# Attention sums and outputs stored from SyncE's queue, and two portions of a unit put inside the attention's first and third quarter

## The chip, the cores and the metric

The kernel runs on 1 core of one Trainium2 chip. The metric is the device time of the program in microseconds (us). The kernel before takes 651.97 us, the median of 3 runs (651.77 to 652.3).

## What is computed

One layer of a hybrid block over 1024 latent tokens and 256 context tokens of width 1024. Cut to what matters:

```python
h  = rmsnorm(x, norm_g) * (1 + scale) + shift          # scale, shift, gate = silu(c) @ w_ada + b_ada
hc = rmsnorm(ctx, norm_g) * (1 + scale_c) + shift_c
q, k, v, za, u, bg, cg, zc = split(h @ w_in)           # eight groups of 512 columns
kc, vc = split(hc @ w_in[:, 512:1536])
# 8 heads of 64: q, k normalised; 8x16 clamped window with a bias table, rotary on latent scores,
# all 256 context keys in the same softmax
attn = neighbourhood_attention(q, k, v, kc, vc, rpb) * silu(za)
conv = bg * conv3(cg * u) * silu(zc)
x_new = x + gate * (concat([attn, conv]) @ w_out)
```

Everything is float32. A product is made of three matmuls (high by high, high by low, low by high), for which each operand is split into a rounded high part and the rest.

## The kernel before, in words

**Stages.** The program first makes the modulated rows `h` (held on the chip as pairs of high and low, tiles `h`), then projects q, k and v in 32 tiles of 128 tokens (`proj_tile`, tile `pacc`) and spills them to DRAM. The attention follows, and then the output projection (`pout`, lines 74 to 76 by way of `out_mm`). The other columns of the input projection (`za`, and `u`, `cg`, `zc`, `bg` of the convolution) are not a stage of their own. They are 16 units of 128 columns, which fill TensorE in and around the attention.

**A unit** (`unit`, lines 338 to 363) is a product of 128 columns with all 1024 tokens: two halves of 512 tokens, each a PSUM bank `pu` (tag U, two banks) that eight steps of k accumulate. Two steps of k, six matmuls of 128x512, are one *portion*; a unit has eight. `next(fill)` issues one portion and stops ahead of the next. With its first portion a unit loads the weights of the next one (`unit_load`, two tiles `uraw` of 256 KB, SyncE's queue), and with its fourth and sixth it queues their splits into `uh` (on ScalarE) and `ul` (on VectorE). The end of a unit queues what is done with its result: for the four `za` units and the `zc` units a SiLU (`silus`, tile `zs`), for the others products of the convolution on VectorE.

**The attention** (lines 1267 to 1295) is a software pipeline of 36 calls of `quarter(n)`, n from 0 to 35. A head has four quarters. In quarter n TensorE makes the scores of quarter n (`pss` against latent keys, `pc` against context keys), the maxima of quarter n-2 are turned and spread (two transposes of `mx` into `pmx`, a VectorE maximum `rm`, two transposes that spread `rm`, a ScalarE copy `mg`), the exponentials of quarter n-2 are taken (`phc`, `phl` and their rests `plc`, `pll`), and the products with v of quarter n-3 are made (`po`). `e = n - 2` and `o = n - 3` are the two older quarters, and `live` says whether such a quarter exists. So quarters 0 and 1 have no maxima to turn, and quarters 0 to 2 have no products with v.

Portions lie between these: one after the exponentials are issued, and `TICKS[n] - 1` more at the end of the quarter, 3 a quarter in most. Ahead of the attention 8 portions have been issued; what is left after quarter 35 is issued in one row (line 1289), ahead of the output projection.

**The order on each engine.** Within the attention the program order of TensorE, ScalarE, VectorE and GpSimd is kept (`strict`, class `ordered`); DMA issues of ScalarE are free of that chain, and SyncE's queue is not in the list, so a scheduler orders its DMAs. [...]

**The stores.** When the last product with v of a bank of 512 queries is issued, `finish` (lines 1019 to 1024) copies the bank `po` (64 rows of outputs and one row of sums) into `ob`, of which there is one buffer, and stores the sums to `rs_d` (2 KB) and the outputs to `o_d` (128 KB). There are 16 such pairs of stores, in quarters 5, 7, 9 and so on. Both are issued from ScalarE. The sums of a pair of heads come back on SyncE's queue (`gated`, line 1250) to be inverted, and the last pair's on GpSimd's queue (`recip`, line 501).

## Time and profile before

| | |
|---|---|
| time, median of 3 runs | 651.97 us |
| the profiled execution: its own time, and the span of its trace | 651.68 us, 649.9 us |
| TensorE busy | 629.0 us, 97% of the span |
| VectorE, ScalarE, GpSimd busy | 431.9, 322.6, 129.4 us |
| moved by DMA | 125.46 MB, mean 193 GB/s |
| the attention in the span | about 279 to 543 us; the output projection starts at 558.22 us |

Times in the trace count from the start of the span. PE is TensorE, PEld its weight loads, DVE VectorE, ACT ScalarE, POOL GpSimd; SPq and ACTq are the queues on which SyncE and ScalarE issue DMAs. A row of a timeline has start, duration, engine, line, operation, output<-input, shape and count, and in brackets how long the engine sat idle before it and what ended that. Busy matmuls are counted to their modelled ends, so that a short wait can lie under the tail of the matmul ahead of it.

### The profile page before, as it was taken

The numbers are of one execution on the slowest core, as the hardware profiler recorded it, in microseconds if no ns is written. First come the engines' busy times: TensorE is split into PE (matmuls) and PEld (weight loads), VectorE is DVE, ScalarE is ACT, GpSimd is POOL, SyncE is SP. The second block draws the span as 40 slices with busy tenths as digits, with TensorE's granted clock in tenths as the row PEclk, the third lists the DMA queues.
The fourth block names the chain that finished last, engine by engine and source line by source line (L and its number), as shares of the span: only waits on it lengthen the run. The fifth ranks groups of instructions, "written<-read, shape, count | busy, mean of one in ns | idle before, by whom it ended". The sixth has DMA issues, their size and how long they took to land.

```text
span 649.9 us, 10273 instructions
## 1 busy us (share of the span) xinstructions
PE 629.0 (97%) x3469; PEld 539.2 (83%) x3469; DVE 431.9 (66%) x814; ACT 322.6 (50%) x693; POOL 129.4 (20%) x137
## 2 busy tenths in 40 slices
PE   5799999999999999999999999999999999999997
PEld 1467799899899999977877888888888888888885
DVE  1557774966684856457786889988998864575111
ACT  3466653442553635428677558565685645352000
POOL 1203203312222132101121111111211111004321
PEclk9799999999999999999999999999999999999999
DMA  8854637686686898789939576886782223966521
GB/s 321 314 179 166 168 105 243 202 263 196 196 278 177 251 262 254 187 228 218 241 103 238 145 179 191 211 213 153 207 190 75 74 75 118 324 222 222 178 102 50
DMA packets 118864, 125.46 MB, mean 193 GB/s; under 512 B 32817, under 2 KB 89353, under 8 KB 117532
## 3 DMA queue, kind: packets, MB, share of 16 engines
q1 hardware_dynamic: 112348, 113.23, 60.9%
q10 hardware_dynamic: 6208, 11.05, 5.3%
q0 software_dynamic: 256, 0.54, 0.3%
q8 instruction: 27, 0.44, 0.3%
q14 instruction: 25, 0.20, 0.1%
HBM read 88.01 MB, written 38.53 MB: 195 GB/s over the span
## 4 chain that ended last, share of the span: by engine, by line
PE 72%; DMA 7%; DVE 7%; ACT 5%; SPq 4%; issue 2%; POOL 1%; ACTq 0%; DVEq 0%; POOLq 0%
PE pu L55 22%; PE pacc L55 17%; PE po L55 5%; PE pout L74 4%; PE pout L75 4%; PE pout L76 4%; SPq L55 3%; PE tr L55 3%; PE cacc L55 3%; PE pss L55 2%; PE pmx L55 2%; DMA v<-v_d 2%; DMA k_s<-k_d 2%; PE pc L55 2%; DVE mx L55 2%
## 5 line engine op out<-in xcount | busy, mean ns | idle before, releaser
L55 PE MATMUL pu<-h,uh 128*128 128x512 f32 x544 | 169.0, 392 | 0.0
L55 PE MATMUL pacc<-wh,h 128*128 128x384 f32 x512 | 135.1, 338 | 0.0
L55 PEld LDWEIGHTS pu<-h,uh 128*128 128x128 f32 x544 | 98.2, 188 | 17.0
L55 PE MATMUL pu<-h,ul 128*128 128x512 f32 x272 | 106.3, 391 | 0.0
L55 PEld LDWEIGHTS pacc<-wh,h 128*128 128x128 f32 x512 | 92.9, 188 | 0.1
L55 POOL TENSOR_TENSOR plc<-sc,phc 128x512 fp32r<-128x512 f32 x32 | 42.5, 1328 | 221.9 <-ACT sc L55 113.2
L55 PE MATMUL pacc<-wl,h 128*128 128x384 f32 x256 | 85.6, 335 | 0.0
L55 POOL TENSOR_TENSOR ss<-ss,few 128x4 f32<-128x4 f32 (+1 forms) x40 | 42.0, 1051 | 126.9 <-DVE ss L55 126.5
L55 PEld LDWEIGHTS pu<-h,ul 128*128 128x128 f32 x272 | 51.1, 188 | 11.2
L55 DVE TENSOR_TENSOR mx<-mx,sb 128x384 f32<-128x384 f32 (+1 forms) x64 | 55.1, 869 | 2.0
L75 PE MATMUL pout<-wol,yh 128*128 128x512 f32 x128 | 49.8, 389 | 0.0
L76 PE MATMUL pout<-woh,yl 128*128 128x512 f32 x128 | 49.6, 389 | 0.0
L74 PE MATMUL pout<-woh,yh 128*128 128x512 f32 x128 | 48.3, 389 | 0.0
L55 PEld LDWEIGHTS pacc<-wl,h 128*128 128x128 f32 x256 | 48.1, 188 | 0.1
L55 DVE TENSOR_REDUCE ss<-sq 128x4 f32<-128x260 f32 (+1 forms) x40 | 15.7, 393 | 46.0 <-ACT sq L55 45.0
L55 ACT COPY mg<-pmx 128x256 f32<-128x256 f32 x32 | 12.0, 374 | 57.8 <-PE pmx L55 47.2
L55 ACT ACTIVATE sq<-pacc 128x256 f32<-128x256 f32 x32 | 12.3, 386 | 53.1 <-PE pacc L55 52.3
L1355 DVE TENSOR_TENSOR ot<-pout,gate 128x512 f32<-128x512 f32 x16 | 10.8, 688 | 40.2 <-PE pout L76 37.7
L55 DVE TENSOR_TENSOR pll<-sb,phl 128x768 fp32r<-128x768 f32 (+2 forms) x33 | 29.3, 889 | 7.9 <-ACT sb L55 7.9
L1356 POOL TENSOR_TENSOR ot<-ot,xr 128x512 f32<-128x512 f32 x15 | 19.6, 1315 | 68.6 <-DVE ot L1355 67.6
L55 DVE TENSOR_TENSOR sc<-sc,mg 128x512 f32<-128x512 f32 x32 | 21.8, 683 | 17.1 <-ACT mg L55 17.1
L55 ACT ACTIVATE qn<-pacc,ss 128x64 f32<-128x64 f32 x128 | 30.1, 330 | 6.0 <-POOL ss L55 3.2
(146 smaller groups left out, 1276.0 us busy)
## 6 DMA issues: line engine op xcount, KB each, us to landing
uraw<-in_w_in SPq DMA_DIRECT2D x34, 256.0 KB
q_d<-qs SPq DMA_DIRECT2D x64, 128.0 KB
k_s<-k_d SPq DMA_DIRECT2D x16, 512.0 KB
q_s<-q_d SPq DMA_DIRECT2D x32, 256.0 KB
wr<-in_w_in SPq DMA_DIRECT2D x40, 192.0 KB
slab<-in_w_ada SPq DMA_DIRECT2D x6, 1024.0 KB
t_d<-btw SPq DMA_DIRECT2D x8, 576.0 KB
bt<-t_d SPq DMA_DIRECT2D x8, 576.0 KB
```

Of the source, the lines that this page charges most:

```text
L55: i = emit(*a, **kw)
L74: i = pe.matmul(ps, ah, bh, start=first, stop=False)
L75: pe.matmul(ps, ah, bl, start=False, stop=False)
L76: pe.matmul(ps, al, bh, start=False, stop=last)
L1355: dve.tensor_tensor(ot, ps, gate[:, cols], ALU.mult)
L1356: (dve if (nh, t) == (1, NB - 1) else pool).tensor_tensor(ot, ot, xr, ALU.add)
```

## The change

The two stores of `finish` are issued by SyncE in place of ScalarE. In quarter 2 (the only one that turns maxima and has no product with v yet) a portion stands between the transposes of `mx` and those of `rm`. In quarter 0 a portion stands between the latent scores and the context scores. `TICKS` stays, so all later portions stand two places earlier, and two fewer are left after quarter 35.

```diff
@@ finish
             act.copy(ob[0:HD + 1], self.po[bank][0:HD + 1])
-            act.dma_start(rs_d[self.p][self.s, bank:bank + 1], ob[64:65])
-            act.dma_start(o_d[self.p][64 * self.s:64 * self.s + 64, bank * 512:(bank + 1) * 512], ob[0:64])
+            sp.dma_start(rs_d[self.p][self.s, bank:bank + 1], ob[64:65])
+            sp.dma_start(o_d[self.p][64 * self.s:64 * self.s + 64, bank * 512:(bank + 1) * 512], ob[0:64])
@@ quarter
         if gating and next(gating[0], "end"):
             gating.clear()
         if live(e):
+            if not live(o):
+                next(fill)
             for i in range(2):
                 pe.transpose(pm[:, 256 + i * P:256 + (i + 1) * P], rm[:, i:i + 1].broadcast_to([P, P]), ident)
             act.copy(mg[:, g * 256:(g + 1) * 256], pm[:, 256:512])
         now = pair_of(n)
         for i, hd_, j in now:
             hd_.scores(j, sbank[:, i])
+        if n == 0:
+            next(fill)
         if live(n):
             heads[n // 4].ctx_scores(n % 4)
```

## The prediction

> **What bounds the kernel now.** I read the page first: busy shares and the granted clock.

> ```profile
> span 649.9 us, 10273 instructions
> PE 629.0 (97%) x3469; PEld 539.2 (83%) x3469; DVE 431.9 (66%) x814; ACT 322.6 (50%) x693; POOL 129.4 (20%) x137
> ...
> PE   5799999999999999999999999999999999999997
> ...
> PEclk9799999999999999999999999999999999999999
> ```

> TensorE is busy for 97% of the span at full granted clock, and the few slices that are not full lie at the two ends. So the kernel is bound by TensorE's instruction stream, and a change can gain only where TensorE stands idle, or by taking matmuls away. This change takes none away. The next view is the windows, cut at the stages.

> ```profile
> 277.00:293.00 16.00, 14.43 (x77) 12.15 (x76) 8.43 (x17) 4.60 (x9) 0.00 (x0) 1.00 0.91 230
> 293.00:365.00 72.00, 69.03 (x389) 56.54 (x388) 56.59 (x86) 52.65 (x84) 13.53 (x12) 1.00 0.79 192
> 365.00:541.00 176.00, 175.72 (x1012) 149.54 (x1011) 153.98 (x236) 108.74 (x180) 29.17 (x26) 1.00 0.61 156
> 541.00:600.00 59.00, 59.00 (x264) 48.86 (x263) 33.15 (x51) 22.70 (x37) 10.46 (x12) 1.00 0.69 229
> ```

> The second number is the length, the third TensorE's busy time. Its idle time is 1.57 us in the attention's first three quarters, 2.97 us in the next 72 us, 0.28 us in the remaining 176 us, and nothing at the start of the output projection. The whole attention holds 4.82 us to be won. The third view, the timeline, says what the idle time waits for.

> ```profile
> 279.26 0.48 PE L55 MATMUL pss<-q_s,k_s 128*128 128x256 f32 x2
> 280.80 0.74 PE L55 MATMUL pc<-q_s,kc_s 128*128 128x256 f32 x4 [1.05 <-DVE qs L55]
> ...
> 289.40 0.38 PE L55 MATMUL pmx<-ci,mx 128*128 128x128 f32 x2
> 290.29 0.43 PE L55 MATMUL pmx<-ci,rm 128*128 128x128 f32 x2 [0.52 <-DVE rm L55]
> ```

> These two waits are the 1.57 us of the first window. In quarter 0 the context scores wait for VectorE to finish with the banks they need. In quarter 2 the spreading transposes wait for the maximum of the transposes just made. They are exactly where the change puts its portions.

> **The portions.** The chain of waits shows what a portion costs, in the row that is left at the end:

> ```profile
> 543.41 14.97 PE pu L55 x66
> ```

> That is eleven portions of six matmuls, 14.97 / 11 = 1.36 us each. In quarter 0 the two `pss` matmuls, half as wide as a portion's, take 1.36 / 6 = 0.23 us together (an estimate). A portion from 279.49 ends at 280.85, and `pc` starts 0.05 us later than before, so 1.31 of 1.36 us is hidden. In quarter 2 between 0.52 us (the idle time shown) and 0.89 us (all the way from 289.40 to 290.29) is hidden; I take 0.66, since the transposes' own issue lies in the 0.89. As `TICKS` stays, two portions fewer follow quarter 35, where TensorE has no idle time and each costs its full 1.36 us. So the two together win 1.31 + 0.66 = **1.97 us**. The idle rows give 1.05 + 0.52 = 1.57 us, less, because they begin only at the modelled tail of the matmul ahead.

> The moved portions need their operands earlier:

> ```profile
> 275.06 0.65 ACT L55 ACTIVATE zs<-pu 128x512 f32<-128x512 f32 x1
> 276.58 1.29 DVE L55 TENSOR_TENSOR ul<-uraw,uh 128x512 fp32r<-128x512 f32 x2
> 278.89 0.60 ACT L55 ACTIVATE zs<-pu 128x512 f32<-128x512 f32 x1 [3.19 <-PE pu L55]
> 288.36 0.62 ACT L55 CAST uh<-uraw 128x512 fp32r<-128x512 f32 x1 [2.27 <-DMA uraw<-in_w_in]
> 290.76 0.37 ACT L55 COPY mg<-pmx 128x256 f32<-128x256 f32 x1 [1.78 <-PE pmx L55]
> ```

> The weights' low parts are ready at 277.87, and the two banks are free at 275.71 and 279.49. The next unit's second split moves from quarter 2 to the end of quarter 1, right behind the cast at 288.36. If its weights land 1 to 2 us after the first ones, the 1.78 us for which ScalarE idles ahead of `mg` covers it. I count nothing.

> **The stores.** Sixteen pairs leave ScalarE's queue. [...]

> ```profile
> 334.53 0.62 ACT L55 CAST uh<-uraw 128x512 fp32r<-128x512 f32 x1
> 334.66 0.22 ACTq L1023 DMA_DIRECT2D rs_d<-ob  x1
> 334.92 0.45 ACTq L1024 DMA_DIRECT2D o_d<-ob  x1
> 335.05 0.62 ACT L55 CAST uh<-uraw 128x512 fp32r<-128x512 f32 x1
> ```

> [...]

> ```profile
> 317.61 0.56 ACT L55 COPY ob<-po 65x512 f32<-65x512 f32 x1
> ...
> 319.87 0.49 ACTq L1023 DMA_DIRECT2D rs_d<-ob  x1
> ...
> 322.19 0.53 ACTq L1024 DMA_DIRECT2D o_d<-ob  x1
> 322.81 0.37 ACT L55 COPY mg<-pmx 128x256 f32<-128x256 f32 x1 [2.24 <-DMA v<-v_d]
> ...
> 349.28 0.56 ACT L55 COPY ob<-po 65x512 f32<-65x512 f32 x1
> ...
> 352.96 0.37 ACT L55 COPY mg<-pmx 128x256 f32<-128x256 f32 x1 [3.12 <-DMA k_s<-k_d]
> ```

> What TensorE paid for these two stands one quarter later:

> ```profile
> 325.00:333.00 8.00, 7.03 (x39) 5.43 (x39) 6.37 (x11) 4.99 (x9) 2.00 (x2) 1.00 0.27 68
> ...
> 357.00:365.00 8.00, 7.80 (x45) 6.39 (x44) 7.90 (x13) 5.82 (x11) 1.31 (x1) 1.00 0.48 131
> ```

> It is 0.97 and 0.20 us, together 1.17. Without DMAs in ScalarE's queue these waits cannot come. The other 1.80 us of that window have other causes: a table load of 1.28 us before each SiLU and another after it, and VectorE late with `mx`. The first SiLU stays at the end of quarter 2, the second moves from quarter 5 (beside a copy of `ob`) to quarter 4 (beside none), the third from quarter 8 to quarter 7 (beside one). I take that as even, and of the 1.17 us I count **1.0 us** won. The bounds are 2.97 + 0.28 us won, if all of this idle time goes, and as much lost again, if the third SiLU's quarter becomes what quarter 5 was.

> SyncE gets the 32 issues, 0.22 + 0.45 us a pair as above, 16 x 0.67 = 10.7 us in all, and a new wait: the first store of a pair waits for the copy of `ob`. Behind it in the changed order stand loads of `v`, the next `uraw`, and `q_s` and `k_s` of a later head.

> ```profile
> 316.27 3.00 SPq L946 DMA_DIRECT2D v<-v_d  x2
> 322.05 0.81 SPq L495 DMA_DIRECT2D zs_d<-zs  x2
> 322.95 1.42 SPq L948 DMA_DIRECT2D v<-vc_d  x2
> 324.46 1.05 SPq L946 DMA_DIRECT2D v<-v_d  x2
> 330.70 1.09 SPq L939 DMA_DIRECT2D kc_s<-kc_d  x2
> ```

> At the first pair SyncE is busy with `v` until 319.27, after the copy has ended at 318.17, so it waits for nothing; and it stands free from 325.51 to 330.70. Loads have that much room and I count nothing. If the room were gone, a `uraw` late by a pair's 0.67 us would hold ScalarE for as long.

> **The tail.** With two portions fewer in the row, the weights and gated outputs for the projection have less time.

> ```profile
> 557.95 0.69 DVE L1311 TENSOR_TENSOR wol<-woraw,woh 128x512 fp32r<-128x512 f32 x1 [0.71 <-ACT woh L1310]
> 558.22 1.75 PE L74 MATMUL pout<-woh,yh 128*128 128x512 f32 x7
> ...
> 563.29 0.69 DVE L1311 TENSOR_TENSOR wol<-woraw,woh 128x512 fp32r<-128x512 f32 x1
> ```

> Each of the eight row groups feeds 18 matmuls, 18 x 0.227 = 4.1 us (1.36 / 6 each). The second group's weights are ready at 558.64 and needed at 562.3, the third's at 563.98 and needed at 566.4: 2.4 us of room. The last unit's SiLU follows the last copy of `ob` at once now, where it waited for the end of its unit. I estimate that the chain of loads behind it loses about 1 us against TensorE, which the room covers. I count **0.2 us** lost, between 0 and the 1.0 us by which the third group would miss if its weights slipped by the two portions' 2.72 us and one more product of 0.69 us.

> **The sum** is -1.97 - 1.0 + 0.2 = -2.8 us (-2.77). The profiled execution took 651.68 us and gives 648.9; the median of the runs is 0.29 us above it, so **649.2 us**, 0.4% faster. A measurement can tell about 0.2%, 1.3 us, from no change.

> **Rivals.** *Stores behind loads, and one `ob`* (slower). In the chain of waits, loads take

> ```profile
> 310.85 11.32 DMA v<-v_d
> ...
> 341.56 10.84 DMA k_s<-k_d
> ```

> from issue to landing in full stretches. A store issued by SyncE stands behind them, and the next copy into `ob` must wait until it has landed. Copies come at 317.61, about 334 and 349.28, some 15 us apart, so the mechanism decides from a store that lands 15 us after its copy: with SyncE's 322.19 and another 10.84 us it would be 333.0, 1 us short. In the case above 2.24 us of ScalarE's wait cost TensorE 0.97 us, 0.43 of it. If seven of the copies wait 2 us each, that is 7 x 2 x 0.43 = 6.0 us, and with the 1.97 us won 656.0 us. Against it: the DMA share is 0.27 in the window from 325, so the backlog is gone before the next copy. Chance 0.15. [...]

> *Given back* (within 0.2%). The portions are won at the start, but the shifted units put their splits and products into other quarters, and the tail runs out of room. In the changed order VectorE takes the last unit's second product ahead of the second group's weights, and so waits for the end of the row before it makes them. With the tail's 1.0 us, and 1.0 us of new waits where 1.0 us was to be won, it is -1.97 + 2.0, or 652.0 us. Chance 0.17.

> *The portions find no gap* (within 0.2%): an operand or a bank isn't ready, and TensorE waits with the portion instead. The rows at 276.58 and 278.89 speak against it; 651.0 us with the stores' gain alone. Chance 0.02.

> **How the numbers follow.** The forecast has 0.66. It runs from 646.8 (651.97 - 1.97 - 2.97 - 0.28) to 650.7. The range goes on to 651.9, into the case that gives the gain back, and leaves out the slower rival and a little of that case, under 2 in 10. Faster is the forecast, 0.66; the same is 0.17 + 0.02; slower is 0.15.

> **What would show it.** In the changed profile `pc` of quarter 0 should start within 0.2 us of 280.80 with a portion ahead of it, and the spreading transposes of quarter 2 should wait for nothing. `mg` should show no wait on a load, and the idle time of TensorE from 293 to 365 should be near 2 us. The row ahead of the projection should have 54 matmuls, and `pout` start near 555.3. Waits of `ob` on its stores would prove the slower rival; idle time ahead of `pout` matmuls the one that gives back.

## The result, and the profile after

The changed kernel takes **671.03 us**, the median of 4 runs (670.37 to 672.67), beside 651.87 us for the kernel before (4 runs, 650.16 to 652.3). The ratio is 1.0314, with an interval of 1.0288 to 1.0341: 3.1% slower, where 0.4% faster was forecast, and far outside the range of 646.8 to 651.9. The profiled execution took 670.98 us.

The page of the changed kernel, busy shares and the granted clock:

```profile
span 669.2 us, 10274 instructions
...
PE 634.8 (95%) x3469; PEld 542.7 (81%) x3469; DVE 431.5 (64%) x814; ACT 323.3 (48%) x693; POOL 129.9 (19%) x137
...
PE   5899999999999999979999997999979999999997
...
PEclk9799999999999999989999998999979999999999
```

TensorE has the same 3469 matmuls. Three new holes stand in its line, and under each the granted clock falls, which before it did not do once inside the attention. The waits of TensorE in the attention, grouped (total in us, times, longest), name what is behind the holes: the portions wait for `zs`, the SiLU on ScalarE. No such wait existed before.

```profile
PE pu L55 <- ACT zs L55: 13.6, 4, 4.6
PE pmx L55 <- DVE rm L55: 3.1, 6, 0.9
```

The windows, cut as before:

```profile
277.00:293.00 16.00, 16.00 (x85) 13.59 (x83) 8.32 (x17) 5.29 (x10) 0.00 (x0) 1.00 0.90 233
293.00:365.00 72.00, 64.03 (x365) 53.84 (x364) 50.95 (x79) 48.57 (x77) 12.25 (x11) 0.98 0.74 179
365.00:541.00 176.00, 167.05 (x938) 141.12 (x938) 147.97 (x224) 102.68 (x170) 28.38 (x25) 0.97 0.59 151
541.00:600.00 59.00, 57.01 (x268) 46.32 (x267) 29.71 (x48) 25.73 (x42) 6.03 (x8) 1.00 0.55 179
```

In the first window the change does what was forecast: the 1.57 us of idle time are gone. Then 7.97 us are idle where 2.97 were, 8.95 where 0.28 were, and 1.99 where nothing was. The column ahead of the last two is the granted clock: 0.98 of 72 us and 0.97 of 176 us, so 1.4 + 5.3 = 6.7 us of clock are lost too.

The first hole, in the timelines of TensorE and of ScalarE:

```profile
288.68 0.38 PE L55 MATMUL pmx<-ci,mx 128*128 128x128 f32 x2
288.82 0.70 PE L55 MATMUL pu<-h,uh 128*128 128x512 f32 x2
...
290.29 0.38 PE L55 MATMUL pmx<-ci,rm 128*128 128x128 f32 x2
...
292.86 0.39 PE L55 MATMUL pu<-h,ul 128*128 128x512 f32 x1
...
297.81 1.22 PE L55 MATMUL pu<-h,uh 128*128 128x512 f32 x2 [4.56 <-ACT zs L55]
```

```profile
290.71 0.37 ACT L55 COPY mg<-pmx 128x256 f32<-128x256 f32 x1 [1.90 <-PE pmx L55]
...
292.51 1.28 ACT L55 ACT_TABLE_LOAD   x1
...
295.86 1.28 ACT L55 ACT_TABLE_LOAD   x1
297.16 1.08 ACT L55 ACTIVATE zs<-pu 128x512 f32<-128x512 f32 x2
```

The moved portion of quarter 2 sits in its gap, and the spreading transposes at 290.29 wait for nothing. But the portion behind the exponentials, whose last matmul starts at 292.86, is now the 16th, the last of a unit. The next portion opens a new unit and needs a `pu` bank. Both banks are held by the unit that has just ended, and each is free only when the SiLU of its half has read it. ScalarE issues that SiLU at the end of the quarter, behind `mg`, the context scores' copy, the exponentials and two table loads. TensorE stands still from 293.25 (292.86 + 0.39) to 297.81.

In the kernel before the same unit ended with the last portion of quarter 2, and the products with v and the scores of quarter 3 lay between it and the next portion. Its two rows for this place, first ScalarE's, then TensorE's next portion:

```profile
297.73 1.09 ACT L55 ACTIVATE zs<-pu 128x512 f32<-128x512 f32 x2
```

```profile
298.64 0.63 PE L55 MATMUL pu<-h,uh 128*128 128x512 f32 x2
```

The first of the two SiLUs ends at about 298.3 and the portion starts at 298.64: it was in time by 0.3 us.

`TICKS` had the units end with quarters, as the sum of its entries shows. With the 8 portions ahead, quarters 0 to 2 bring it to 16, quarters 3 to 5 to 24, 6 to 8 to 32, 9 to 16 to 56, and 17 to 26 to 88: these are the ends of the units with a SiLU, each at a quarter's end, and only the one at 120 lies beyond. Two portions more ahead of it put the ends at 16, 56 and 88 on the portion behind the exponentials, inside a quarter; 24 falls by luck on the end of quarter 4 and 32 on that of quarter 7, and 120 on that of quarter 35, where the row follows at once. Measured from one start of a matmul to the next, less its usual step, the four stalls are 4.72, 4.42, 3.78 and 1.38 us.

After each of the first three stalls the clock drops. The windows of the first one and after it (the clock is the third number from the end):

```profile
293.00:298.00 5.00, 0.44 (x3) 0.20 (x2) 2.29 (x5) 4.90 (x8) 1.26 (x1) 0.95 1.08 191
298.00:301.40 3.40, 3.40 (x9) 2.66 (x10) 0.00 (x0) 0.24 (x1) 0.00 (x0) 0.57 0.77 158
301.40:305.00 3.60, 3.60 (x25) 3.26 (x24) 1.56 (x3) 0.68 (x2) 0.00 (x0) 1.00 0.95 279
```

Nine matmuls are recorded in the 3.4 us behind the stall and 25 in the next 3.6 us. The trace's record of the clock has 13.65 us at half inside the attention, 6.8 us of work lost.

The sum closes. From the first `pss` matmul to the first of `pout` there were 278.96 us (279.26 to 558.22), and now there are 296.76 (278.50 to the row below).

```profile
575.26 1.75 PE L74 MATMUL pout<-woh,yh 128*128 128x512 f32 x7
```

That is 17.80 us more: 14.30 of stalls and 6.8 of clock, less some 3 won. From there to the end of the span it was 91.68 us and is 93.94, 2.26 more. The attention starts 0.76 us earlier. 17.80 + 2.26 - 0.76 = 19.30, the difference of the spans (669.2 - 649.9).

### The profile page after: what moved, and what is told of

It reads as the page before. It is cut to its first block, busy times and chain, and to the rows that moved or that the text cites. A ratio compares the mean times of both kernels' runs of the same rounds, so it can differ in the third digit from the quotient of the medians.

```text
span 669.2 us, 10274 instructions
## 1 busy us (share of the span) xinstructions
PE 634.8 (95%) x3469; PEld 542.7 (81%) x3469; DVE 431.5 (64%) x814; ACT 323.3 (48%) x693; POOL 129.9 (19%) x137
## 4 chain that ended last, share of the span: by engine, by line
PE 65%; DMA 10%; ACT 8%; DVE 8%; SPq 3%; issue 2%; POOL 1%; ACTq 0%; DVEq 0%; POOLq 0%
PE pu L55 21%; PE pacc L55 17%; PE po L55 5%; SPq L55 3%; DMA woraw<-in_w_out 3%; PE cacc L55 3%; PE tr L55 3%; PE pout L74 2%; PE pss L55 2%; PE pout L76 2%; PE pout L75 2%; PE pc L55 2%; PE pmx L55 2%; DMA k_s<-k_d 2%; ACT L55 2%
## 5 line engine op out<-in xcount | busy, mean ns | idle before, releaser
L55 PE MATMUL pu<-h,uh 128*128 128x512 f32 x544 | 173.6, 401 | 13.6 <-ACT zs L55 13.6
L55 PE MATMUL pacc<-wh,h 128*128 128x384 f32 x512 | 135.4, 338 | 0.1
L55 PEld LDWEIGHTS pu<-h,uh 128*128 128x128 f32 x544 | 100.4, 193 | 32.7 <-ACT zs L55 15.2
L55 PE MATMUL pu<-h,ul 128*128 128x512 f32 x272 | 108.5, 399 | 0.0
L55 PEld LDWEIGHTS pacc<-wh,h 128*128 128x128 f32 x512 | 92.9, 188 | 0.5 <-ACT qn L55 0.5
L55 POOL TENSOR_TENSOR plc<-sc,phc 128x512 fp32r<-128x512 f32 x32 | 43.1, 1346 | 240.9 <-ACT sc L55 144.1
L55 PE MATMUL pacc<-wl,h 128*128 128x384 f32 x256 | 85.6, 335 | 0.0
L55 POOL TENSOR_TENSOR ss<-ss,few 128x4 f32<-128x4 f32 (+1 forms) x40 | 42.0, 1051 | 127.8 <-DVE ss L55 127.5
L55 PEld LDWEIGHTS pu<-h,ul 128*128 128x128 f32 x272 | 52.3, 192 | 11.9
L55 DVE TENSOR_TENSOR mx<-mx,sb 128x384 f32<-128x384 f32 (+1 forms) x64 | 55.2, 870 | 2.0
L55 PEld LDWEIGHTS pacc<-wl,h 128*128 128x128 f32 x256 | 48.1, 188 | 0.1
L74 PE MATMUL pout<-woh,yh 128*128 128x512 f32 x128 | 46.3, 392 | 1.4 <-ACT woh L1314 0.8
L55 DVE TENSOR_REDUCE ss<-sq 128x4 f32<-128x260 f32 (+1 forms) x40 | 15.7, 393 | 46.4 <-ACT sq L55 45.5
L55 ACT COPY mg<-pmx 128x256 f32<-128x256 f32 x32 | 12.0, 374 | 64.9 <-PE pmx L55 64.9
L55 ACT ACTIVATE sq<-pacc 128x256 f32<-128x256 f32 x32 | 12.3, 386 | 53.0 <-PE pacc L55 52.2
L55 DVE TENSOR_TENSOR pll<-sb,phl 128x768 fp32r<-128x768 f32 (+2 forms) x33 | 28.8, 874 | 12.2 <-ACT sb L55 12.2
L55 DVE TENSOR_REDUCE rm<-pmx 128x2 f32<-128x256 f32 x32 | 13.5, 423 | 32.9 <-PE pmx L55 32.9
L55 ACT ACTIVATE qn<-pacc,ss 128x64 f32<-128x64 f32 x128 | 30.1, 330 | 6.3 <-POOL ss L55 3.2
```

The source lines that it names most:

```text
L55: i = emit(*a, **kw)
L74: i = pe.matmul(ps, ah, bh, start=first, stop=False)
```

## The experiments

**Theory A**: two portions placed early let every later portion stand two places earlier; units whose end feeds a SiLU then end inside a quarter; the next portion waits for the bank behind ScalarE's whole chain; and each long wait costs clock on top. **Rivals**: the stores on SyncE hold something up (B); each moved portion costs its share, wherever units end (C); the places of the two portions are themselves at fault (E); the first stall drags the others behind it (D). In each expectation the letters are as given there. Lengths of the attention below are from the first `pss` to the first `pout` matmul of the profiled run.

### The stores alone

```diff
-            act.dma_start(rs_d[...], ob[64:65])
-            act.dma_start(o_d[...], ob[0:64])
+            sp.dma_start(rs_d[...], ob[64:65])
+            sp.dma_start(o_d[...], ob[0:64])
```

> The stores issued by SyncE, the portions as before. Theory A (the added portions push the end of a unit into the middle of a quarter, where the next unit's first portion waits for the SiLU that frees its bank): the stores cost nothing, 651 us, between 649.5 and 652.5, and ScalarE's waits on loads ahead of mg (2.2, 2.4 and 3.1 us) are gone. Theory B (stores behind loads on SyncE's queue hold up the attention): most of the 19 us is here, 662 to 671 us.

Measured: 649.27 us (9 runs) beside 652.0; ratio 0.9957 (0.9941 to 0.9973). The attention is 276.60 us long, 2.36 less than before. SyncE's queue and ScalarE around the first pair:

```profile
316.85 2.39 SPq L946 DMA_DIRECT2D v<-v_d  x2
319.90 0.25 SPq L1023 DMA_DIRECT2D rs_d<-ob  x1
322.17 0.47 SPq L1024 DMA_DIRECT2D o_d<-ob  x1
```

```profile
318.36 0.56 ACT L55 COPY ob<-po 65x512 f32<-65x512 f32 x1
...
321.21 0.38 ACT L55 COPY mg<-pmx 128x256 f32<-128x256 f32 x1
```

The stores leave at 319.90 and 322.17, as late as before (319.87 and 322.19), but now it is SyncE that is held up, while ScalarE goes on by way of a SiLU to `mg` at 321.21, with no idle time ahead of it (322.81 before, behind 2.24 us). The stores are a gain, and not the cause of the loss.

### The portions alone

```diff
 against the changed kernel
-            sp.dma_start(rs_d[...], ob[64:65])
-            sp.dma_start(o_d[...], ob[0:64])
+            act.dma_start(rs_d[...], ob[64:65])
+            act.dma_start(o_d[...], ob[0:64])
```

> The two portions, the stores issued by ScalarE as before. Theory A: all of the loss is here, 669 to 674 us, with waits of pu on zs of about 4 us in quarters 2, 16 and 26. Theory B: 650 to 652 us, the waits of TensorE in quarters 0 and 2 gone and nothing in their place.

Measured: 671.45 us (4 runs), ratio 1.0308 (1.0283 to 1.0333), with stalls of 4.72, 4.42, 3.90 and 1.38 us at the same four unit ends. The whole loss is in the portions; B is out.

### One portion, so that the shift is one

```diff
 against the kernel before, in quarter
         if live(e):
+            if not live(o):
+                next(fill)
```

> Only the portion of quarter 2 is added, stores by ScalarE as before: every later portion stands one place earlier and not two. Theory A: the units with a SiLU then end in the middle of quarters 2, 5, 8, 16 and 26, five places in place of three, so half the change costs more than all of it: five times 4.3 us of wait and 1.6 us at a lower clock, about 680 us (672 to 688). Rival C (what costs is the moved work itself, so much for each portion moved): about half of the loss, 661 us.

Measured: 670.13 us (4 runs, 667.53 to 674.46), ratio 1.0285 (1.0248 to 1.0322). Half of the moved portions cost as much as both. With a shift of one, the ends at 24 and 32 cross their quarters too, and there are five stalls (3.88, 3.63, 3.18, 2.86 and 2.25 us, 15.8 in all), and 20.5 us at half clock. The number of places was as Theory A had it. The price of one was not, and the time lies below the 672 to 688 us expected. All five stalls are shorter than the 4.3 us assumed; that the units end one portion later against ScalarE's chain fits this, and the first stall of the shift alone, below, shortens in the same way. Rival C, which had 661 us, falls.

### Both portions, the quarters evened out

```diff
 against the changed kernel
-TICKS = [2, 3, 3, 3, 3, 2, ...
+TICKS = [1, 3, 2, 3, 3, 2, ...
```

> The changed kernel with one portion less at the end of quarters 0 and 2 (TICKS 1 and 2 in place of 2 and 3), so that all units end where they did before. Theory A: the waits of pu on zs are gone, TensorE's waits in quarters 0 and 2 too; 649.5 us, between 647.5 and 651.5. Theory B: as slow as the changed kernel but for a few us, 662 to 671 us.

Measured: **648.36 us** (8 runs), ratio 0.9958 (0.994 to 0.9975). Its windows:

```profile
277.00:293.00 16.00, 16.00 (x85) 13.72 (x84) 8.99 (x18) 6.00 (x10) 0.00 (x0) 1.00 0.90 234
293.00:365.00 72.00, 68.96 (x402) 57.63 (x401) 57.95 (x87) 52.78 (x87) 13.37 (x12) 1.00 0.80 191
```

Two entries of a table take the kernel from 3.1% slower to 0.4% faster. No wait on `zs` and no halved clock is left. The portions stand at the same places as in the changed kernel, so their places were never at fault. But 3.04 us are idle in the second window, where the stores alone leave 1.74; the sixth and seventh experiments go after that.

### The shift taken back one quarter later

```diff
 against the changed kernel
-TICKS = [2, 3, 3, 3, 3, 2, ...
+TICKS = [2, 3, 3, 1, 3, 2, ...
```

> The changed kernel, but quarter 3 issues one portion in place of three, so that from the end of quarter 3 on each portion stands in the quarter in which it stood in the kernel before; only the unit that ends inside quarter 2 still ends ahead of its quarter's end. Theory A (each such unit end has its own price: the next portion waits for the SiLU, and the clock is then halved for a window): one stall near 293 of 4.7 us, one half-clock window of 3.4 us that costs 1.7, none at 405, 489 and 563; 648.4 us (both portions in place and no such unit end) + 6.4 = 654.8, between 653 and 657. Rival D (the first stall sets ScalarE behind TensorE, and the later stalls only follow from the first): stalls stay at 405 and 489, and the time is near 671.

Measured: 659.04 us (7 runs, 656.26 to 659.93), ratio 1.0104 (1.0073 to 1.0134). The waits of TensorE:

```profile
PE pu L55 <- ACT zs L55: 4.6, 1, 4.6
```

One stall is left, at its place and with its size, and the other three are gone. So each has its own price, and D is out. The time is 4 us above the 654.8 us expected, and outside 653 to 657. The traced execution is the fastest of the seven, 656.26 us, and it shows a part that the expectation had left out: quarter 3 with a single portion has nothing to cover its own waits (1.19, 1.02 and 1.12 us between 305 and 311), and they halve the clock for a second window. Its attention is 284.75 us long, 8.77 more than in the evened-out kernel: TensorE is idle for 5.45 us more between 277 and 365 (8.49 against 3.04, less than its stall and three waits together, as the evened-out kernel has waits of its own there), and 3.4 us of clock are lost. What makes the median another 2.8 us longer than this execution is in no trace.

### The evened-out order with the stores on ScalarE

```diff
 against the evened-out kernel
-            sp.dma_start(rs_d[...], ob[64:65])
-            sp.dma_start(o_d[...], ob[0:64])
+            act.dma_start(rs_d[...], ob[64:65])
+            act.dma_start(o_d[...], ob[0:64])
```

> Both portions in place, quarters 0 and 2 one portion shorter at their ends so that every unit ends with its quarter as before, and the stores left on ScalarE: the portions' own gain without the stores' and without the unit ends. The prediction's term, 1.97 us won: 650.0. If the portion of quarter 2 only moves its idle time into a later wait (1.5 us ahead of a product with v in quarter 3, seen once with the stores on SyncE), 1.31 + 0.66 - 1.5 = 0.5 won: 651.5. If the waits on the stores in ScalarE's queue eat the rest: 652 or more.

Measured: 651.63 us (12 runs) beside 652.31 (26 runs); ratio 0.9979 (0.9956 to 1.0003), so a gain isn't certain. The attention is 277.77 us long, 1.19 less than before, where 1.97 was the term. The rest is given back behind the portions, in the window from 293:

```profile
293.00:365.00 72.00, 67.66 (x388) 56.02 (x387) 57.02 (x86) 52.48 (x84) 13.27 (x12) 1.00 0.76 192
```

4.34 us are idle there, 1.37 more than before.

### The portion of quarter 0 alone, evened out

```diff
 against the changed kernel
-TICKS = [2, 3, 3, 3, 3, 2, ...
+TICKS = [1, 3, 3, 3, 3, 2, ...
@@ quarter
         if live(e):
-            if not live(o):
-                next(fill)
```

> Stores on SyncE, the portion inside quarter 0 alone, taken from the end of the same quarter; quarter 2 as before. By the prediction's terms the portion of quarter 0 is worth 1.31 us beside 649.3 with the stores alone: 648.0. If the portion of quarter 2 is worth its 0.66, this kernel is 0.7 slower than the one with both (648.4): 649.0. If that portion only brings the new wait of 1.5 us in quarter 3, this one is the fastest: about 647.5.

Measured: **647.77 us** (12 runs, 646.47 to 651.31), ratio 0.994 (0.9918 to 0.9961), the lowest here. The attention is 275.17 us long: 1.43 less than with the stores alone, and 0.81 less than with both portions. So in these traces the portion of quarter 2 costs 0.81 us. The intervals of the two kernels overlap, and which is faster is settled only as far as single traces settle it. The mechanism shows in the kernel with both, on TensorE and then on ScalarE and GpSimd:

```profile
293.33 0.46 PE L55 MATMUL po<-phc,v 128*65 128x256 f32 x2
295.14 0.34 PE L55 MATMUL po<-plc,v 128*65 128x256 f32 x1 [1.34 <-POOL plc L55]
```

```profile
289.36 0.37 ACT L55 COPY mg<-pmx 128x256 f32<-128x256 f32 x1 [1.79 <-PE pmx L55]
...
293.12 0.63 ACT L55 ACTIVATE sc<-sc 128x512 f32<-128x512 f32 x1
```

```profile
293.83 1.26 POOL L55 TENSOR_TENSOR plc<-sc,phc 128x512 fp32r<-128x512 f32 x1 [25.17 <-ACT sc L55]
```

Quarter 2 is bound by the chain from the spreading transposes over `mg`, the context scores' copy, a table load and the exponentials to `plc`. A portion ahead of the spreading transposes starts that chain 0.7 us later (`mg` stands 10.87 us behind the first `pss` here, 10.19 with quarter 0's portion alone, 289.12 - 278.93), and the portion missing at the end of the quarter lets TensorE come to `plc` sooner. The first product with v does come 0.59 us earlier (14.85 against 15.44 us behind the first `pss`), and then 1.34 us are spent waiting.

### Exp in place of SiLU

```diff
 against the changed kernel
-            act.activation(out[half], ps, AF.Silu)
+            act.activation(out[half], ps, AF.Exp)
```

> The changed kernel with Exp in place of SiLU inside the attention (the gate values are not SiLU's, that part of the computation is replaced): ScalarE then has no table to switch between the exponentials and the unit's end. Theory A with the table loads as part of the wait: the stall at 293 loses both loads of 1.28 us (4.7 to 2.2), those at 405, 489 and 563 one each (4.4 to 3.1, 3.8 to 2.5, 1.4 to 0.1), 6.4 us in all: 664.6 if the half clock follows the shorter stalls too, and down to 658 if it doesn't. If the wait were for something else than ScalarE's order (the next unit's weights, the queue), the stalls and the 671 us stay.

The gates' values are then not SiLU's; only the time is of interest. Measured: 659.06 us (4 runs), ratio 1.0112 (1.0062 to 1.0163), 12 us less than the changed kernel. The stalls are 1.89, 3.01 and 2.36 us, and the fourth is gone: shorter by 2.83 (two table loads), 1.41, 1.42 and 1.38. So what TensorE waits for is ScalarE's chain up to the SiLU, and each table load in it, 1.28 us long in the rows of the changed kernel, costs some 1.4 us.

The rest of the 12 us is clock. TensorE's three waits, and a window of one clock step behind each:

```profile
296.40 0.74 PE L55 MATMUL pu<-h,uh 128*128 128x512 f32 x2 [1.73 <-ACT zs L55]
...
402.66 1.16 PE L55 MATMUL pu<-h,uh 128*128 128x512 f32 x2 [2.84 <-ACT zs L55]
...
485.16 0.73 PE L55 MATMUL pu<-h,uh 128*128 128x512 f32 x2 [2.20 <-ACT zs L55]
```

```profile
296.94:300.35 3.41, 3.41 (x20) 2.81 (x19) 0.72 (x2) 0.00 (x0) 0.00 (x0) 1.00 1.21 178
402.75:406.16 3.41, 3.41 (x8) 2.65 (x9) 0.65 (x1) 0.34 (x1) 0.00 (x0) 0.50 1.16 263
484.66:488.07 3.41, 2.91 (x13) 2.34 (x14) 1.76 (x3) 0.94 (x2) 0.18 (x1) 1.00 0.87 235
```

Only the longest wait halves the clock: 3.41 us at half in place of 13.65, 5.1 us won.

### The shift without the portions inside

```diff
 against the kernel with the stores alone
-TICKS = [2, 3, 3, 3, 3, 2, ...
+TICKS = [3, 3, 4, 3, 3, 2, ...
```

> Stores on SyncE, no portion inside a quarter; quarters 0 and 2 each issue one portion more at their ends, so that all later portions stand two places earlier, as in the changed kernel. Theory A (the shift against the quarters costs, wherever the two portions stand): the units of portions 16, 56, 88 and 120 end ahead of a portion again; the first stall is one portion (1.36 us) shorter than in the changed kernel, near 3.4 us, the others as there (4.4, 3.8, 1.4), three or four half-clock windows: 649.3 with the stores alone + 13 + 5 to 7 + 1 to 2 in the output projection, 668 to 671. Rival E (the portions inside quarters 0 and 2 are at fault, by their place): 649 to 650.

Measured: 673.15 us (4 runs, 671.27 to 674.4), ratio 1.0324 (1.0275 to 1.0373), 2 us above the 668 to 671 expected. No added portion stands inside a quarter, and the loss is all there:

```profile
PE pu L55 <- ACT zs L55: 12.3, 4, 4.3
```

The stalls are 3.37, 4.43, 3.81 and 1.37 us, the first shorter by one portion, as expected, and 13.65 us are at half clock. Together with the evened-out kernel this settles Theory A from both sides, and E is out: with the added portions at their places and no shift there is no loss; with the shift and no added portion inside a quarter there is the whole loss.

### The short row alone

```diff
 against the kernel with the stores alone
-... + 3 * [3] + [4, 4, 3, 2]
+... + 3 * [3] + [4, 4, 3, 4]
```

> Stores on SyncE, nothing else but quarter 35, which issues two portions more, so that two fewer are left in the row ahead of the output projection: the tail's term alone. The prediction took 0.2 us for it (0 to 1.0): 649.5. In the changed kernel the last SiLU's wait shows 1.4 us and the output projection is 2.3 us longer, 0.9 with the stores on ScalarE: if that comes from the short row, 649.3 + 1.4 + 0.9 to 2.3 = 651.6 to 653.0.

Measured: 649.65 us (4 runs), ratio 0.9967 (0.992 to 1.0015). The attention is 276.54 us long and the rest 91.69, both as with the stores alone. Two portions fewer in the last row cost nothing, so the output projection's 2.26 us in the changed kernel do not come from the short row, and the expectation's 651.6 to 653.0 us are out. Nor does the unit of portion 120 stall here, though it ends with quarter 35 as in the changed kernel. Three portions lie here between the last product with v and its end, at 540.00 to 544.1 us, so that ScalarE has copied `ob`, loaded a table and finished the first SiLU (540.20 to 543.21) before the next portion needs the bank. In the changed kernel one portion lies there: the unit ends at 563.04 us and the first SiLU at 564.20, and the fourth stall is 1.38 us.

The traces show where the 2.26 us arise. In the chain that ended last in the changed kernel, the load that brings back the last sums of the softmax (`ri`, GpSimd's queue) takes 4.50 us, and VectorE waits for it, with the products of the last unit and the splits of the projection's weights behind it in its order. With the short row alone VectorE waits 6.39 us for it, until 544.35; in the changed kernel the wait is 9.21. The first row below is of that chain, the second is VectorE's, both in the changed kernel.

```profile
563.74 4.50 DMA ri<-rs_d
```

```profile
568.26 0.25 DVE L55 RECIPROCAL ri<-ri 128x16 f32<-128x16 f32 x1 [9.21 <-DMA ri<-rs_d]
```

The low parts of the second row group's weights are ready 3.23 us behind the first `pout` matmul in the changed kernel, and 0.41 us behind it before. The same goes for all twelve kernels. In four of them (the changed one, the portions alone, the shift alone, Exp) the first load of `tb` for the projection is issued 0.65 to 0.67 us ahead of this load, which then takes 3.49 to 5.37 us, and the projection is 0.91 to 2.43 us longer. In the other eight it is issued 0.7 to 2.1 us behind, the load of the sums takes 2.04 to 2.19 us, and the projection is as long as before (91.67 to 91.69 us). The order and the longer load go together in every trace; no run changed that order alone.

## Why the prediction was wrong, point by point

**The step that failed** stands in "The portions", in the paragraph on the operands of the moved portions: "the two banks are free at 275.71 and 279.49 ... I count nothing." It asked whether the two portions that are put into gaps find their banks, and they do. It did not ask it of the portions that the shift pushes across the end of a unit. The sentence "As `TICKS` stays, two portions fewer follow quarter 35" took the shift as a gain at the end alone. The runs show in its place 14.3 us of waits for a bank, 6.8 us of clock and 2.3 us in the output projection. Without the shift (the evened-out kernel) all three are gone and the time is 648.36 us, inside the forecast range and 0.8 us below the forecast; that it comes so close is in part luck, since the stores won more than their term and the portion of quarter 2 lost.

**The SiLUs**, of which it says "I take that as even": the prediction had the shift in hand ("the second moves from quarter 5 ... to quarter 4"), yet it weighed it only for what it does to ScalarE, and by quarters. Counted in portions, the first SiLU's unit ends two portions ahead of its quarter's end. It is still issued at the end of quarter 2, as the prediction says, and that is why TensorE waits.

**The portions' own gain** was right where the chain was TensorE's: 1.31 us for quarter 0. With the quarters evened out, `pmx` of quarter 2 stands 8.82 us (portion of quarter 0 alone) and 8.85 us (both) behind the first `pss`, where it was 10.13: 1.31 and 1.28. For quarter 2, 0.66 was counted and 0.59 measured at the first product with v; but 1.34 us came back as a wait on `plc` in the next quarter. The end of that chain, not the gap inside it, decides.

**The stores** were sized at 1.0 us from what TensorE lost behind ScalarE's two waits ahead of `mg`, 2.24 and 3.12 us long, which end with transfers of `v` and `k_s`. Alone they shorten the attention by 2.36 us, more than twice the term, and the span by 1.6 (649.9 - 648.3), inside the bounds of 3.25 us either way. The direction was right, and so was the cause as far as the rows go: ScalarE has no wait on a load ahead of `mg` any more. What made ScalarE wait for these transfers, no run shows.

**The tail** was counted at 0.2 us, at most 1.0. The short row alone bears this out, but in the changed kernel 2.26 us are lost there. The prediction had seen that the last unit's SiLU no longer waits for the end of its unit, and had asked only what the chain of loads behind it loses against TensorE. That these loads are then issued ahead of the load of the last sums was not in the sum.

**The rivals**: the one for slower had the chance 0.15 and the wrong mechanism. No copy into `ob` waits for its stores: ScalarE's waits with the stores alone have one row on `ob`, and it is on TensorE.

```profile
ACT mg L55 <- PE pmx L55: 53.1, 26, 3.4
...
ACT ob L55 <- PE po L55: 3.0, 1, 3.0
```

Whether a store on SyncE's queue lands only behind the loads issued ahead of it, no run shows: with the stores alone the first store is issued at 319.90, behind `v` at 316.85, and no row shows when it landed. (The prediction's rows of before have `zs_d` at 322.05 behind `v` at 316.27 in the same way; that landing isn't recorded either.) No wait of TensorE on a transfer is left with the stores alone, where before has one of 0.2 us (on `v`). Of the rival that gives back, the order it named is there, but it is a small part of the loss: in the changed kernel VectorE's product at 575.47 us, ahead of the second group's weights, waits 0.71 us for the end of the row.

**What would have shown it**: the two rows of before at 297.73 and 298.64. A portion that starts 0.3 us after the SiLU that frees its bank has no room to come a portion earlier.

## What to carry to other kernels

When filler work is moved forward, check the whole sequence behind it: every place where a filler changes its buffer must still lie behind the instruction that frees that buffer. A table of counts such as `TICKS` can hold that alignment without naming it, so take a moved piece out of the same stage's count first, and change the total only as a separate step. And a gap in the engine that bounds the kernel is worth filling only if the chain that comes out of the stage isn't started later by the filling.

## What the runs showed of the hardware

```profile
344.93:348.35 3.42, 1.47 (x8) 0.81 (x6) 3.38 (x7) 3.34 (x5) 1.35 (x3) 1.00 0.96 240
348.35:351.76 3.41, 2.35 (x6) 1.87 (x7) 0.39 (x1) 1.48 (x3) 0.00 (x0) 0.50 1.08 279
...
495.12:498.53 3.41, 1.32 (x6) 0.77 (x6) 3.02 (x5) 3.35 (x6) 1.29 (x1) 1.00 0.52 140
498.53:501.94 3.41, 3.41 (x11) 2.72 (x11) 0.37 (x2) 0.24 (x1) 0.00 (x0) 0.50 0.77 251
```

The wait of 2.20 us in the kernel with Exp is longer than the second of these, but it straddles two windows, and the clock stayed (the row from 484.66 above). The first of the two:

```profile
481.25:484.66 3.41, 1.71 (x9) 1.00 (x8) 3.38 (x6) 2.45 (x5) 1.09 (x1) 1.00 0.70 193
```

Between these lie two windows that went different ways: of the kernel with the portions alone, where the next window kept its clock, and of the fifth experiment, where three separate waits added up and it did not.

```profile
405.19:408.60 3.41, 1.55 (x9) 0.89 (x7) 3.38 (x7) 2.40 (x4) 1.04 (x1) 1.00 0.89 231
408.60:412.01 3.41, 1.01 (x4) 0.86 (x5) 1.71 (x3) 2.81 (x4) 0.22 (x1) 1.00 1.11 313
```

```profile
308.15:311.57 3.42, 1.60 (x13) 1.34 (x13) 1.33 (x3) 1.41 (x3) 0.81 (x1) 1.00 0.00 0
311.57:314.98 3.41, 3.41 (x12) 2.68 (x11) 3.38 (x7) 2.48 (x4) 0.63 (x1) 0.50 0.54 142
```

So in these rows the windows in which TensorE is busy for 1.47 and 1.32 us of 3.41 are followed by one at half clock, which costs 1.7 us (half of 3.41), and the one with 1.71 us is not. Of the two between them the one with 1.55 us is not and the one with 1.60 us is, so no limit can be read from them, as the ends of matmuls are modelled. This is said of windows at full clock. Windows at half clock went differently: the one from 348.35 above, with 2.35 us busy, was followed by another at half, and so was the one from 492.05 in the changed kernel, with 2.05 us. The window that precedes a halving need not be wholly idle: 1.95 us of 3.42 were enough in the one from 344.93.
